# Unused pieces in the SBUF pools: the operands of TensorE at other byte positions against the weights

## The chip, the cores and the metric

The kernel runs on one core of a Trainium2 chip. The metric is the device time of one execution in microseconds (us); for the kernel before it is 1540.58 us, the median of three runs from 1537.99 to 1541.2. Engines are named as in the profile: PE is TensorE (matmuls), PEld its weight loads, DVE VectorE, ACT ScalarE, POOL GpSimd, SP SyncE, which issues the DMAs.

## The reference: one step of a decoder layer

64 sample tokens and 1024 prompt tokens go through one layer with a model width of 1024, in float32:

```
h = RMSNorm(x);  [q|k|v|gu|gv|ga|gb] = h @ w_in
A = sliding-window attention(q, k, v, sinks)          # window 128, 16 heads of 64, 4 KV heads
B = gelu(gu) * (tril(W_s) @ LayerNorm(gelu(gv)) + b)  # chunks of 128 positions, 6 groups
x = x + (sigmoid(ga) * (A @ w_pa) + sigmoid(gb) * (B @ w_pb)) @ w_out
z = RMSNorm(x) @ w_up                                 # 2 x 2816 columns
x = x + (gelu(conv3(z)_a) * conv3(z)_b) @ w_down;  y = RMSNorm(x)
```

Beside y, the newest keys, values, convolution rows and gate rows are returned.

## The kernel before

Every large product is done three times in a reduced-precision form: each float32 operand is split in a high and a low part (`split`, line 39: a cast on ACT, a subtraction on DVE), and PE adds high*high, high*low and low*high into one PSUM bank. So a weight piece has the tiles wh and wl, an activation has th and tl (or hh and hl, mh and ml, oh and ol, s). PE reads the weights as the stationary operand, 128 columns of four bytes in each partition (a weight load, PEld), and the activation as the moving operand, of 256, 288, 320 or 512 columns. Each matmul has a weight load of its own, which runs beside the matmul before it.

The tokens lie in two groups. Group 0 has 576 columns (64 samples and 512 prompt tokens), group 1 has 512. Where both halves of a pair of weight blocks meet both halves of a group, seven products of a Strassen-like scheme take the place of eight (class `Chain`, line 249): each operand tile then holds seven combinations of 288 columns (group 0) or of 256 (group 1), and one product j is four steps kk of three matmuls, twelve in all, with the weights wh[kk], wl[kk] (the matmul at line 295).

The stages in order of time, from the profile's timeline:

- 0 to 115 us, line 511: v and gate columns by tokens; the weights are moving here (tile w2h, w2l, 256 columns), the activations hh and hl stationary.
- 115 to 468 us, line 295: the "pairs" q, k, gu, ga, gb by `Chain`. Group 0's operands are the tiles T0h (288 columns), group 1's the tiles T1h (256). The first three pairs run for group 0 alone, then both groups alternate with each product's weights, and at the end the first three run for group 1 alone.
- 468 to 822 us: attention (lines 1155, 1182, 1206), with the branch and merge products at line 238 between its steps, and then w_out, also line 238. Group 0 runs there in two chunks of 320 and 256 columns, group 1 in one of 512. The operand tiles are in the pools mlp0, act0, hm0 (group 0) and mlp1, act1, hm1 (group 1).
- 822 to 1292 us, line 295 again: the up products. Group 0's operands are the tiles T0 (288 columns), group 1's T1 (256). Three of the 22 pairs of blocks run for group 0 alone at the start, and for group 1 alone among the others.
- 1292 to 1530 us, line 1651: the down products, 288 and 256 columns of one tile in turn, three matmuls each; at the end the final norm and y.

What sets the order: each engine runs its instructions in the order in which the code issues them; the class `Weights` (line 78) issues loads, splits and sums of the weights a fixed number of pieces ahead of PE (`get`, line 219). SBUF is given out by pools: a pool stands as one block of bytes in each partition, opened at the left or (`side="right"`) at the right end of what is free, and its tiles stand one behind another. So an unused tile in a pool moves what is allocated behind it. Where a new tile takes bytes that an older tile had, its first writer waits for the older one's last users.

The lines that the change touches are the pools c1 (line 464), wide (line 496), T0h (tiles at line 648), kv (line 902), mlp1 (line 977), T0 (tiles at line 1407) and T1 (line 1449).

Of the kernel before, what the change touches and what calls it, by code (L numbers as in the profile page):

```python
# [6 lines left out]
F32 = mybir.dt.float32  # L7
# [8 lines left out]
P = 128  # L16
# [18 lines left out]
def layer(tc, a):  # L35
# [3 lines left out]
    def split(hi, lo, src, pin=False):  # L39

        for x in (S.copy(hi, src), V.tensor_sub(lo, src, hi.bitcast(F32))):  # L41
            if pin:
                tc.keep_in_program_order(x)
# [5 lines left out]
    with ExitStack() as top:  # L49
# [191 lines left out]
        W = Weights(top.enter_context(tc.tile_pool(name="wp", bufs=2)), 4, 4)  # L241
        W.sm = top.enter_context(tc.tile_pool(name="sm", bufs=2))

        tx = [{}, {}]
        tops = ExitStack()

# [2 lines left out]
        def right(stack, name, bufs=1):  # L249
            return stack.enter_context(tc.tile_pool(name=name, bufs=bufs, side="right", reuse_waits="tile"))  # L250
# [110 lines left out]
        with ExitStack() as ph1:  # L361
            c1 = ph1.enter_context(tc.tile_pool(name="c1", bufs=1))
# [31 lines left out]
            wide = {}  # L394
# [68 lines left out]

            rstg = [c1.tile([P, len(gr["toks"])], F32, name=f"rst{gr['g']}") for gr in groups]
            lnst = c1.tile([P, 9, 3, 6], F32, name="lnst")
            pso = ExitStack()
            psa = pso.enter_context(tc.tile_pool(name="psa", bufs=7, space=PSUM))

# [25 lines left out]
            gvp = pa0.enter_context(tc.tile_pool(name="gvp", bufs=4))  # L494
            hp1 = pa0.enter_context(tc.tile_pool(name="hs1", bufs=1))
            wide["pool"] = pa0.enter_context(tc.tile_pool(name="wide", bufs=2))
            hp0 = right(hs0o, "hs0")
            rsg = [pool.tile([P, gr["n"]], F32, name=f"rs{gr['g']}") for gr, pool in zip(groups, (c1, hp1))]
            hs = [[], []]
# [123 lines left out]
            t0h, xr = right(th0, "T0h"), right(xro, "xr")  # L623
# [11 lines left out]
            def sums_of(g, kk):  # L635
                x_in(4 * g + kk + 1)
                n2, x = groups[g]["n"] // 2, xin.pop(4 * g + kk)
                for e in range(2):
                    k = kk + 4 * e
                    V.scalar_tensor_tensor(x[:, e], x[:, e], gains[:, 0, k:k + 1], rsg[g], ALU.mult, ALU.mult)  # L640
                t4 = xr.tile([P, 4, 288], F32, name="t", bufs=2)[:, :, :n2]
                combine(t4, *(x[:, e, n2 * h:n2 * h + n2] for e in range(2) for h in range(2)), eng=V)
                return x[:, 0, 0:n2], t4, x[:, 1].rearrange("p (h c) -> p h c", h=2)

            def t0_job(kk):
                def go():
                    first, t4, rest = sums_of(0, kk)
                    txa[0][kk] = th, tl = tuple(t0h.tile([P, 7, 288], F32R, name=f"t{y}{kk}") for y in "hl")
                    split(th[:, 0], tl[:, 0], first)
                    split(th[:, 1:5], tl[:, 1:5], t4)  # L650
                    split(th[:, 5:7], tl[:, 5:7], rest)
                return go

            def t1_job(kk):
# [6 lines left out]

            none = lambda: None
            jobs = [lambda: x_in(0)] + [x for kk in range(4) for x in (t0_job(kk), none)] + [t1_job(kk) for kk in range(4)]
            tokens(1, ("v", 1), lambda i, ps: v_out(1, i, ps), jobs, lambda: stats_tok(1))
            stats_all(1)
# [224 lines left out]
            kvo, kvp = ExitStack(), {}  # L890
# [3 lines left out]
            def operands(gr, kv):  # L894

                def go():
                    if kv == NKV:
                        if gr["g"] == 0:
                            operands(groups[1], 0)()
                        return  # L900
                    g, n = gr["g"], gr["n"]
                    at, nk = ((NS, 512), (448, 640))[g]
                    t = kvp["p"].tile([P, 2, 640], F32R, name="kst", bufs=2)[:, :, :nk]
                    gr["kst"][kv] = t
                    r = 64 * (kv % 2)
                    for o in (0, 64):
                        nc.sync.dma_start(t[o:o + 64].bitcast(F32), kd[kv // 2][r:r + 64, :, at:at + nk])
                    for c in (2 * kv, 2 * kv + 1):
                        q = gr["qt"][c] = kvp["p"].tile([P, 2, 512], F32R, name="q", bufs=4)
                        nc.sync.dma_start(q.bitcast(F32), qd[g][c][:, :, gr["soff"]:n])  # L910
                return go

            def prepare(gr):

                g = gr["g"]
                gr["kvo"] = ExitStack()
                vp = (gr["kvo"].enter_context(tc.tile_pool(name="vv0", bufs=1, reuse_waits="tile")) if g == 0
                      else right(gr["kvo"], "vv1"))
                gr["vst"], gr["dvst"] = {}, {}

                def value(name, src, i):
                    def go():
                        t = gr[name][i] = vp.tile([P, NKV, P], F32R, name=f"{name}{i}")
                        nc.sync.dma_start(t.bitcast(F32), src[i])
                    return go

                vs, ds = (((0, 1, 2), (1, 2, 3)), ((3, 4, 5, 6), (4, 5, 6, 7)))[g]
                return [operands(gr, 0)] * (1 - g) + [value("vst", vd, vs[0])] + [
                    x for i in range(len(ds)) for x in (
                        [value("vst", vd, vs[i])] * (i > 0) + [value("dvst", dvd, ds[i])])] + [operands(gr, 1)]  # L930
# [44 lines left out]
            kvp["p"] = kvo.enter_context(tc.tile_pool(name="kv", bufs=1, reuse_waits="tile"))  # L975
            prep = prepare(groups[0])
            m1 = mo[1].enter_context(tc.tile_pool(name="mlp1", bufs=1, reuse_waits="tile"))
            b_order = [(0, 0), (1, 0), (0, 1), (1, 1)] + [(c, g) for c in range(2, KD) for g in range(2)]
            sgs, bst = {}, {}

# [383 lines left out]
            t0p = right(t0o, "T0")  # L1364
# [38 lines left out]
            def t0_split(kk):  # L1403

                def go():
                    x0, x1, t4 = hx.pop(kk)
                    tx[0][kk] = th, tl = tuple(t0p.tile([P, 7, 288], F32R, name=f"t{y}0{kk}") for y in "hl")
                    split(th[:, 0], tl[:, 0], x0[:, 0:288])
                    split(th[:, 5:7], tl[:, 5:7], x1.rearrange("p (h c) -> p h c", h=2))
                    split(th[:, 1:5], tl[:, 1:5], t4)  # L1410
                return go
# [34 lines left out]
        def pool2(name, bufs, **kw):  # L1446
            return ph2.enter_context(tc.tile_pool(name=name, bufs=bufs, reuse_waits="tile", **kw))

        t1p = pool2("T1", 1)
        up = pool2("up", 2)  # L1450
        pse = ExitStack()
        psu = pse.enter_context(tc.tile_pool(name="psu", bufs=8, space=PSUM, reuse_waits="tile"))
# [437 lines left out]
```

## Time and profile before

| What | Value |
|---|---|
| median of three runs | 1540.58 us |
| the profiled execution | 1540.43 us, its span 1538.7 us, 1.7 us around it |
| PE busy | 1524.6 us, 99% of the span, 11528 matmuls |
| weight loads (PEld) | 1483.3 us, 96% |
| DVE, ACT, POOL busy | 1178.6 us (77%), 851.4 us (55%), 267.8 us (17%) |
| DMA | 289.88 MB, 188 GB/s in the mean |
| line 295, all matmuls | 6384 of the 11528 |

The profile's matmul durations run from the start of a matmul to its end in PSUM, and successive matmuls overlap: one of 256 columns is listed with some 0.28 us, and the next starts some 0.12 us later. What a matmul costs the span is the step from its start to the start of the next, so the steps are read from the timeline's start times, or from a stretch of time divided by the matmuls in it.

### The profile page before, as it was taken

The page shows a single profiled execution, that of the slowest core. Times are in us where ns is not written, and L with a number is a line of the kernel's source. Part 1 is how long each engine was busy: PE and PEld are TensorE (multiplying, and loading weights), DVE is VectorE, ACT ScalarE, POOL GpSimd, SP SyncE. Part 2 cuts the span into 40 slices and gives each one's busy share as a digit, 9 for nine tenths or more (in the row PEclk, how much of TensorE's full clock was granted, in tenths as well). Part 3 has the DMA queues.
Part 4 walks back from the last instruction along what each step waited for, and adds up shares of the span by engine and source line. Part 5 has one row for each costly group of instructions (what it writes and reads, how often), then busy time and mean ns, then how long its engine had stood idle before and what let it go on. Part 6 is the DMA issues. An engine that isn't in the chain of part 4 may idle for free.

```text
span 1538.7 us, 30106 instructions
## 1 busy us (share of the span) xinstructions
PE 1524.6 (99%) x11528; PEld 1483.3 (96%) x11528; DVE 1178.6 (77%) x1897; ACT 851.4 (55%) x1767; POOL 267.8 (17%) x382
## 2 busy tenths in 40 slices
PE   9999999999999999999999999999999999999997
PEld 8999999999998989988989999999999999999997
DVE  7798876755576877979568978898898878775686
ACT  7557666653455775764444554655555556453452
POOL 0001000110030222310234222332142222000002
PEclk9999999999999999999999999999999999999999
DMA  7687446764778757449977423332232216973363
GB/s 244 219 270 260 161 161 218 236 212 142 241 237 285 221 165 252 152 140 312 339 255 267 138 109 113 121 120 93 108 128 100 102 62 224 365 252 96 111 183 123
DMA packets 135231, 289.88 MB, mean 188 GB/s; under 512 B 15536, under 2 KB 36848, under 8 KB 135088
## 3 DMA queue, kind: packets, MB, share of 16 engines
q1 hardware_dynamic: 134944, 287.96, 55.3%
q8 instruction: 90, 1.47, 0.4%
q14 instruction: 53, 0.43, 0.1%
q10 hardware_dynamic: 144, 0.01, 0.0%
HBM read 198.97 MB, written 90.92 MB: 188 GB/s over the span
## 4 chain that ended last, share of the span: by engine, by line
PE 87%; DMA 4%; DVE 3%; issue 3%; ACT 2%; POOL 1%; SPq 0%; POOLq 0%; ACTq 0%; DVEq 0%
PE st L295 45%; PE mm L238 16%; PE dn L1651 13%; PE st L511 6%; PE po L1206 2%; PE sc L1155 2%; PE pt L1182 1%; DMA v<-gvd 1%; POOL x L1714 1%; PE mx L793 1%; DMA wl<-upd 1%; DVE wl L41 1%; DMA kd<-q 0%; DMA x<-xt 0%; ACT wh L41 0%
## 5 line engine op out<-in xcount | busy, mean ns | idle before, releaser
L295 PE MATMUL st<-th,wh 128*128 128x288 f32 (+1 forms) x2128 | 616.9, 290 | 1.6 <-ACT k L274 1.2
L295 PE MATMUL st<-tl,wh 128*128 128x288 f32 (+1 forms) x2128 | 615.3, 289 | 0.0
L295 PE MATMUL st<-th,wl 128*128 128x288 f32 (+1 forms) x2128 | 614.4, 289 | 0.0
L295 PEld LDWEIGHTS st<-th,wh 128*128 128x128 f32 x2128 | 402.8, 189 | 3.1 <-ACT k L274 2.2
L295 PEld LDWEIGHTS st<-th,wl 128*128 128x128 f32 x2128 | 402.8, 189 | 0.0
L295 PEld LDWEIGHTS st<-tl,wh 128*128 128x128 f32 x2128 | 402.7, 189 | 0.0
L41 ACT CAST wh<-wraw 128x512 fp32r<-128x512 f32 (+2 forms) x188 | 129.4, 700 | 92.8 <-PE mm L238 41.4
L1651 PE MATMUL dn<-th,wh 128*128 128x288 f32 (+1 forms) x616 | 177.5, 288 | 0.8 <-ACT zb L321 0.6
L1651 PE MATMUL dn<-th,wl 128*128 128x288 f32 (+1 forms) x616 | 177.3, 288 | 0.2 <-DVE wl L41 0.2
L1651 PE MATMUL dn<-tl,wh 128*128 128x288 f32 (+1 forms) x616 | 177.2, 288 | 0.0
L41 DVE TENSOR_TENSOR wl<-wraw,wh 128x512 fp32r<-128x512 f32 (+2 forms) x188 | 148.2, 802 | 24.8 <-ACT wh L41 22.3
L41 DVE TENSOR_TENSOR wl<-ws,wh 128x512 fp32r<-128x512 f32 x168 | 118.5, 716 | 54.2 <-ACT wh L41 53.4
L41 ACT CAST wh<-ws 128x512 fp32r<-128x512 f32 x168 | 102.5, 621 | 91.7 <-PE st L295 63.4
L1651 PEld LDWEIGHTS dn<-th,wh 128*128 128x128 f32 x616 | 115.8, 188 | 1.2 <-ACT zb L321 0.8
L1651 PEld LDWEIGHTS dn<-th,wl 128*128 128x128 f32 x616 | 115.9, 188 | 0.4 <-DVE wl L41 0.4
L1651 PEld LDWEIGHTS dn<-tl,wh 128*128 128x128 f32 x616 | 115.9, 188 | 0.0
L41 ACT CAST th<-traw 128x544 fp32r<-128x544 f32 (+1 forms) x85 | 54.5, 642 | 52.1 <-PE dn L1651 38.5
L511 PE MATMUL st<-w2h,hh 128*128 128x256 f32 x288 | 81.3, 284 | 1.5 <-ACT hh L46 0.7
L511 PE MATMUL st<-w2l,hh 128*128 128x256 f32 x288 | 81.0, 282 | 0.0
L511 PE MATMUL st<-w2h,hl 128*128 128x256 f32 x288 | 80.3, 282 | 0.2 <-DVE hl L47 0.2
L41 DVE TENSOR_TENSOR tl<-traw,th 128x544 fp32r<-128x544 f32 (+1 forms) x85 | 61.0, 721 | 23.1 <-ACT th L41 22.7
L281 POOL TENSOR_TENSOR z<-kn,k 128x288 f32<-128x288 f32 (+1 forms) x32 | 31.1, 975 | 244.0 <-ACT kn L276 236.6
(271 smaller groups left out, 2941.3 us busy)
## 6 DMA issues: line engine op xcount, KB each, us to landing
wraw<-wt SPq DMA_DIRECT2D x137, 512.0 KB
traw<-td SPq DMA_DIRECT2D x77, 272.0 KB
td<-za SPq DMA_DIRECT2D x22, 544.0 KB
q<-qd SPq DMA_DIRECT2D x16, 512.0 KB
upd<-hl SPq DMA_DIRECT2D x14, 512.0 KB
td<-t SPq DMA_DIRECT2D x11, 544.0 KB
wpart<-wt SPq DMA_DIRECT2D x22, 256.0 KB
qd<-q SPq DMA_DIRECT2D x8, 576.0 KB
```

The lines of the kernel that those rows point to most:

```text
L41: for x in (S.copy(hi, src), V.tensor_sub(lo, src, hi.bitcast(F32))):
L238: PE.matmul(ps[:, lo:lo + c1 - c0], u[:, k, :], v[:, c0:c1], start=(k == 0 and i == 0), stop=(k == nk - 1 and i == 2))
L281: op(to, pick(x, to, lo, hi), pick(y, to, lo, hi))
L295: PE.matmul(ps, u[:, kk, :], v, start=first and kk + i == 0, stop=kk == 3 and i == 2, skip_group_check=True)
L511: PE.matmul(ps, u[:, lo:lo + P], v[:, k, :], start=k + i == 0, stop=k == KD - 1 and i == 2)
L793: PE.matmul(ps[:, P * i:P * i + P], vn[:, i], late["wst"][:, c, :], start=True, stop=True)
L1155: PE.matmul(ps[:, h, o0:256], q, kst[kv][:, e, k0:cur + P], start=e == 0, stop=e == 1)
L1182: PE.transpose(pt[:, h * P:h * P + P], s[:, h, 0:P], ident)
L1206: PE.matmul(po, v[:, kv, :], t, start=e == 0, stop=last)
L1651: PE.matmul(place(m, e), u[:, m, :], v[:, lo:hi], start=new and i + k == 0 and (e == 0 or m % 2 == 0), stop=i == NU - 1 and k == 2, skip_g ...
L1714: G.tensor_mul(xc, xc, rs)
```

## The change: unused pieces in seven pools

A helper `line(pool, n)` allocates a tile of n bytes in each partition that nothing reads or writes. It is called once in each of the pools c1 (96 bytes), wide (64), T0h (32), kv (64), mlp1 (64) and T1 (64), and twice in T0 (96 bytes, behind the tiles of kk = 1 and behind those of kk = 3).

```diff
+        gaps = iter(range(99))
+
+        def line(pool, n):
+
+            pool.tile([P, n // 4], F32, name=f"gap{next(gaps)}", bufs=1)
...
             lnst = c1.tile([P, 9, 3, 6], F32, name="lnst")
+            line(c1, 96)
...
             wide["pool"] = pa0.enter_context(tc.tile_pool(name="wide", bufs=2))
+            line(wide["pool"], 64)
...
                     split(th[:, 5:7], tl[:, 5:7], rest)
+                    if kk == 3:
+                        line(t0h, 32)
...
                     gr["kst"][kv] = t
+                    if g == 0 and kv == 0:
+                        line(kvp["p"], 64)
...
             m1 = mo[1].enter_context(tc.tile_pool(name="mlp1", bufs=1, reuse_waits="tile"))
+            line(m1, 64)
...
                     tx[0][kk] = th, tl = tuple(t0p.tile([P, 7, 288], F32R, name=f"t{y}0{kk}") for y in "hl")
+                    if kk % 2:
+                        line(t0p, 96)
...
         t1p = pool2("T1", 1)
+        line(t1p, 64)
         up = pool2("up", 2)
```

The instructions of all engines, their order and their shapes are the same as before. What differs is where tiles stand. In the built programs every weight piece wh, wl of the pool wp starts at a byte position of 32 modulo 128, before and after. The table gives the moving operand's start minus that of the weights of the same matmul, modulo 128 (the "offset" from here on):

| Matmuls | Columns | Count | Offset before | Offset after |
|---|---|---|---|---|
| pairs, T0h (line 295) | 288 | 1344 | 64 | 32 |
| pairs, T1h (line 295) | 256 | 1344 | 96 | 64 |
| up, T0 of kk = 0 and 1 (line 295) | 288 | 924 | 64 | 0 |
| up, T0 of kk = 2 and 3 (line 295) | 288 | 924 | 64 | 96 |
| up, T1 (line 295) | 256 | 1848 | 0 | 64 |
| line 511, group 0, until 80 us | 256 | 480 | 32 | 64 |
| line 511, group 1, from 80 us | 256 | 384 | 0 | 64 |
| line 238, act0 and hm0 | 320 and 256 | 768 | 96 | 64 |
| line 238, mlp1 and hm1 | 512 | 336 | 96 | 64 |
| line 238, mlp0; act1 | 320 and 256; 512 | 288; 192 | 64 | 64 |
| line 1155, kv (scores) | 256 and 128 | 256 | 0 | 64 |
| line 1206, at0; at1 (values) | 512 | 56; 64 | 32; 64 | 96; 96 |
| line 1651, down products | 288 and 256 | 1848 | 64 | 64 |

Since tiles now overlap other older tiles than before, three DMAs on SP differ in what they wait for. On SP in the down products, the load of the first residual tile x, which takes bytes that belonged to the pool up before (names: x1d are the DRAM tiles of the residual, wraw and traw raw weights and activations, td the DRAM tiles of the gated products). Before:

```order
L131 DMA wraw<-wt 128x512 [waits DMAHW7_49]
L1437 DMA traw<-td_72 128x544 [waits DMAHW0_49,Activation_49]
L131 DMA wraw<-wt 128x1024 [waits DMAHW1_49]
L1639 DMA x_16743<-x1d_57 128x544 [waits DMAHW2_49]
L1639 DMA x_16743<-x1d_58 128x544 [waits DMAHW3_49]
```

With the change:

```order
L131 DMA wraw<-wt 128x512 [waits DMAHW7_49]
L1452 DMA traw<-td_72 128x544 [waits DMAHW0_49,Activation_49]
L131 DMA wraw<-wt 128x1024 [waits DMAHW1_49]
L1655 DMA x_16751<-x1d_57 128x544 [waits DMAHW2_49,PE_49]
L1655 DMA x_16751<-x1d_58 128x544 [waits DMAHW3_49]
```

The first of the four pieces of x now also waits for PE: the last 64 bytes of T1 reach into x's place, so PE must have ended the up products. In return two later loads on SP (the tiles a22 of the down weights, line 441 before) no longer wait for PE.

## The prediction

> **What bounds the kernel now.** I read the page's first two parts and its chain first, then the table of waits, then the timeline and stretches of time for the step from one matmul to the next.
>
> ```profile
> span 1538.7 us, 30106 instructions
> PE 1524.6 (99%) x11528; PEld 1483.3 (96%) x11528; DVE 1178.6 (77%) x1897; ACT 851.4 (55%) x1767; POOL 267.8 (17%) x382
> PEclk9999999999999999999999999999999999999999
> PE 87%; DMA 4%; DVE 3%; issue 3%; ACT 2%; POOL 1%; SPq 0%; POOLq 0%; ACTq 0%; DVEq 0%
> PE st L295 45%; PE mm L238 16%; PE dn L1651 13%; PE st L511 6%; PE po L1206 2%; PE sc L1155 2%; PE pt L1182 1%; DMA v<-gvd 1%; POOL x L1714 1%; PE mx L793 1%; DMA wl<-upd 1%; DVE wl L41 1%; DMA kd<-q 0%; DMA x<-xt 0%; ACT wh L41 0%
> ...
> PE st L295 <- ACT k L274: 1.2, 2, 0.9
> PE st L566 <- DVE c_ones L69: 1.2, 1, 1.2
> ```
>
> PE is busy in 99% of the span at the full granted clock, the chain is 87% PE, and the longest waits of PE sum to 1.2 us each. So the span is a sum of PE's steps, and the change can matter only through their length: it adds no instruction and moves none. A step shorter by 1 ns in all 6384 matmuls of line 295 is 6.4 us.
>
> The timeline in the up products, at the borders between group 1's twelve matmuls (256 columns, offset 0) and group 0's (288, offset 64):
>
> ```profile
> 1087.97 0.28 PE L295 MATMUL st<-th,wh 128*128 128x256 f32 x1
> ...
> 1089.41 0.30 PE L295 MATMUL st<-th,wh 128*128 128x288 f32 x1
> 1089.55 0.30 PE L295 MATMUL st<-tl,wh 128*128 128x288 f32 x1
> ...
> 1091.00 0.28 PE L295 MATMUL st<-th,wh 128*128 128x256 f32 x1
> ...
> 1092.43 0.30 PE L295 MATMUL st<-th,wh 128*128 128x288 f32 x1
> ```
>
> Twelve of 256 columns take 1.44 and 1.43 us, 119.6 ns a step. Twelve of 288 take 1.59 us, 132.5 ns. Nothing waits between them, so these are PE's own steps.
>
> Other offsets are found in other stages. Stretches of time with the matmuls in them (each is in flight for about two steps, so a stretch also counts two that began before it; I take two off):
>
> ```profile
> core 0: us, PE busy (x), PEclk, DMA share, GB/s
> 30.00:50.00 20.00, 20.00 (x173) 1.00 0.69 218
> 85.00:112.00 27.00, 27.00 (x228) 1.00 0.87 296
> 120.00:148.00 28.00, 28.00 (x213) 1.00 0.73 245
> 437.00:467.00 30.00, 30.00 (x253) 1.00 0.88 297
> 681.00:724.00 43.00, 43.00 (x186) 1.00 0.88 304
> 727.00:776.00 49.00, 49.00 (x370) 1.00 0.95 334
> 783.00:821.00 38.00, 38.00 (x164) 1.00 0.69 225
> 1300.00:1480.00 180.00, 180.00 (x1445) 1.00 0.62 204
> ```
>
> - 256 columns, offset 32 (line 511, group 0, first row): 20/171 = 117.0 ns.
> - 256 columns, offset 0 (line 511, group 1, second row): 27/226 = 119.5 ns. The same line, shape and weights as the row before; only the activation tile and its offset differ.
> - 288 columns, offset 64 (T0h alone, third row): 28/211 = 132.7 ns.
> - 256 columns, offset 96 (T1h alone, fourth row): 30/251 = 119.5 ns.
> - 512 columns, offset 64 (act1) and 96 (hm1), the rows from 681 and 783: 43/184 = 233.7 and 38/162 = 234.6 ns.
> - 320 and 256 columns in turn, offset 96 (hm0, from 727): 49/368 = 133.2 ns, 266.3 for the two.
> - 288 and 256 in turn, offset 64 (down products, last row): 180/1443 = 124.7 ns, 249.5 for the two.
>
> The last is split by the timeline; the same 320 and 256 columns at offset 64 (mlp0) stand in the chain of waits as a piece without a gap:
>
> ```profile
> 1390.40 0.28 PE L1651 MATMUL dn<-th,wh 128*128 128x256 f32 x1
> ...
> 1390.75 0.30 PE L1651 MATMUL dn<-th,wh 128*128 128x288 f32 x1
> ...
> 1391.15 0.28 PE L1651 MATMUL dn<-th,wh 128*128 128x256 f32 x1
> ...
> 516.60 3.16 PE mm L238 x24
> ```
>
> Three of 256 in 0.35 us are 116.7 ns, three of 288 in 0.40 us 133.3. With 132.3 for 288 (between 131.7, below, and 132.7) the pair of 249.5 leaves 117.2 for 256 at offset 64, which I take. The mlp0 piece is 3.16/24 = 131.7 ns, 263.3 for the two.
>
> So 256 columns take about 117 ns at offsets 32 and 64, and about 119.5 at 0 and 96. The difference holds in stages with a DMA share from 0.3 to 0.9, so I lay it on the position of the operand against the weights that load beside it.
>
> **The change part by part.**
>
> 1. T1 goes from offset 0 to 64: 1848 x (119.6 - 117.2 = 2.4 ns) = 4.4 us saved.
> 2. T1h goes from 96 to 64: 1344 x 2.3 ns = 3.1 us saved.
> 3. Line 511, group 1, from 0 to 64: 384 x 2.3 = 0.9 us saved. Group 0 goes from 32 to 64, 117.0 to 117.2: nothing.
> 4. Line 238, act0 and hm0, from 96 to 64: 133.2 - 131.7 = 1.5 ns on 768, 1.1 us saved. The 336 of 512 columns: 0.9 ns, 0.3 us.
> 5. Scores and values, 376 matmuls with gaps for the softmax between them: at 2.3 ns each either way 0.9 us at most. I take nothing, since PE runs there with other work to fill in.
>
> Together 9.8 us on the side of the gain, nearly all in stretches in which nothing but PE ends last.
>
> 6. The 288-column operands, 3192 matmuls, leave offset 64, where alone the trace shows them. Their price at 32, 0 and 96 must be bounded. Below nothing: a straight line between 256 columns (117.2) and 320 (263.3 - 117.2 = 146.1) at offset 64 gives 131.7 for 288; they now step by 132.6, so a better offset may give 0.9 ns, 2.9 us saved. Above: all of them pay what 256 columns pay at the worse offsets, 2.4 ns, 7.7 us lost. Nearest rows: at 32, the 256 columns of line 511 are as fast as at 64, so T0h's 1344 cost nothing. At 96 the wider operands pay less than 256 columns: of the 2.9 ns that the pair 320 and 256 pays, 2.3 belong to the 256, and 0.6 to the 320; 512 columns pay 0.9. For 288, between 2.3 and 0.6, I take 1.5 ns, at 0 the same for want of a row: 1848 x 1.5 = 2.8 us lost.
>
> Sum: 9.8 - 2.8 = 7.0 us less. Against the profiled execution, 1540.43, that is 1533.4; it stands 0.15 us under the median, so 1533.6 us.
>
> What feeds PE has to keep up. The stage with the least slack for the weights' splits, and SP's queue where the one new wait stands:
>
> ```profile
> core 0: us, PE busy (x) PEld busy (x) DVE busy (x) ACT busy (x) POOL busy (x), PEclk, DMA share, GB/s
> 832.00:1290.00 458.00, 457.58 (x3623) 456.64 (x3622) 390.30 (x564) 250.43 (x497) 128.78 (x187) 1.00 0.32 118
> ...
> 1311.34 0.46 SPq L131 DMA_DIRECT2D wraw<-wt  x1
> 1311.85 2.35 SPq L1639 DMA_DIRECT2D x<-x1d  x4
> 1314.29 1.27 SPq L131 DMA_DIRECT2D wraw<-wt  x2
> ```
>
> DVE is busy 390.30 of 458 us there, 85%; with a stage shorter by 2 us it is 86%. The load of x, with the loads of wraw queued behind it on SP, is issued at 1311.85, some 20 us after the last up product (1292 us), so its wait for PE has ended by then. It would cost something only if SP came to it before PE ended the up products. The two waits that fall away on SP stand 27 us later and are as free.
>
> **The rivals.**
>
> - *288 columns gain as well* (they were at their worse offset): 9.8 + 2.9 = 12.7 us less, 1527.8. For it: 132.6 lies above the line of the other widths. Against: 0 and 96 are the worse ones for 256.
> - *The offset does nothing*; the steps of 117 and 119.5 belong to stages, tiles or neighbours in time, and the change only renames bytes: 1540.5. For it: no trace here shows one tile at two offsets. Against: three stages at the worse offsets agree within 0.1 ns, and two at the better ones. This is also what a rule would give: the Trainium skill, "TensorE: Matmul & The Clock Gate", section "Step-by-step: what each phase is for", says that PE has two independent read ports into SBUF, and that loading the next weights takes no read bandwidth from the running matmul. By that the sum would be 0; the two stretches of line 511 (117.0 and 119.5 ns) disagree with it.
> - *The gain is lost to the producers*: PE catches up with DVE's splits in the up products, which then ends last there; the 4.4 us of T1 are lost, 1538.0. For it: 85% busy. Against: in this trace PE waits for DVE or ACT in line 295 for hardly over 1 us.
> - *Slower: 288 columns pay much more at 0 and 96 than 256 do.* Place: the up products of group 0, 1848 steps. The first of T0's twelve after a T1 block at offset 0 already takes 0.14 us against 132.5 ns for the mean, some 7 ns more. At 7 ns each 12.9 us are lost against 9.8: 1543.7. It decides from 9.8/1848 = 5.3 ns a step. Against: no row of 256, 320 or 512 columns shows more than 2.5 ns between two offsets.
>
> **How the numbers follow.** The forecast, 1530.5 to 1537, has a chance of 0.52; 288 columns gaining 0.18; no effect 0.10; producers 0.12; slower 0.08. The likeliest time is 1533.6. The range runs from 1526 (the first rival, with 256 columns at 116.7) to 1539 (9.8 against the upper bound of 7.7, or the third rival). Less than 0.2% either way can't be told from no change, so faster means under 1537.5: the forecast, the first rival and half of the third, 0.76, and a little of the second's edge, 0.77. Same: the rest of the third and the second, 0.16. Slower: 0.07.
>
> **What would show it.** In the profile of the changed kernel, twelve matmuls of T1 should take 1.41 us in place of 1.44, a stretch of T1h alone 117.2 ns a step, line 511 from 80 us on 117; the pair 320 and 256 of hm0 263.3. A T0h step of 132.5 and T0 steps of 134 carry term 6; T0 blocks under 1.58 us mean the first rival, 1.66 and over the last. The count of matmuls and PE's waits should stay; a wait of line 295 for wl of over 1 us would be the third. The prediction is wrong if the 256-column steps stay at 119.5, or if 288-column steps change by over 2.5 ns.

## The result and the profile after

The changed kernel takes 1528.58 us (median of four, 1527.77 to 1530.25) against 1539.63 us for the kernel before beside it: 0.993 of it, with a 95% interval from 0.9912 to 0.9947. The change makes it faster by about 11 us. Run again beside other kernels it took 1530.48 us, 0.994 (0.9928 to 0.9953).

Lines of the page, and the longest waits of PE, of the changed kernel:

```profile
span 1526.5 us, 30105 instructions
PE 1512.8 (99%) x11528; PEld 1471.7 (96%) x11528; DVE 1178.1 (77%) x1897; ACT 851.3 (56%) x1767; POOL 268.3 (18%) x382
PE 90%; issue 3%; DVE 2%; ACT 2%; DMA 1%; POOL 1%; SPq 0%; POOLq 0%; DVEq 0%; ACTq 0%
...
PE st L574 <- DVE c_ones L69: 1.2, 1, 1.2
PE st L519 <- ACT hh L46: 1.0, 1, 1.0
```

The same matmuls, and PE's busy time is 11.8 us less: 1512.8 for 1524.6. DVE, ACT and POOL are as busy as before. So the steps are shorter, as the prediction had it. Four stretches of time show where, first of the kernel before (us, PE's busy time with the matmuls in it, clock, DMA share, GB/s):

```profile
84.00:110.00 26.00, 26.00 (x219) 1.00 0.89 299
180.00:295.00 115.00, 115.00 (x913) 1.00 0.54 184
860.00:1225.00 365.00, 365.00 (x2902) 1.00 0.30 110
1300.00:1455.00 155.00, 155.00 (x1244) 1.00 0.63 208
```

and of the changed kernel:

```profile
84.00:110.00 26.00, 26.00 (x223) 1.00 0.86 294
180.00:295.00 115.00, 115.00 (x932) 1.00 0.58 194
860.00:1225.00 365.00, 365.00 (x2925) 1.00 0.29 108
1300.00:1455.00 155.00, 155.00 (x1245) 1.00 0.61 201
```

With two matmuls taken off for those in flight, the step falls in line 511 (84 to 110 us) from 119.8 to 117.6 ns, in the pairs (180 to 295, half 288 and half 256 columns) from 126.2 to 123.7, and in the up products (860 to 1225) from 125.9 to 124.9. It stays in the down products, whose tiles stand where they stood. These four rows serve as the measure in all experiments.

What of it lies in 256 and what in 288 columns, the borders of the blocks of twelve in the changed kernel's timeline tell (start, duration, instruction):

```profile
238.04 0.29 PE L301 MATMUL st<-th,wh 128*128 128x256 f32 x1
...
239.43 0.30 PE L301 MATMUL st<-th,wh 128*128 128x288 f32 x1
...
241.02 0.29 PE L301 MATMUL st<-th,wh 128*128 128x256 f32 x1
...
242.40 0.29 PE L301 MATMUL st<-th,wh 128*128 128x288 f32 x1
...
1076.09 0.28 PE L301 MATMUL st<-th,wh 128*128 128x256 f32 x1
...
1077.49 0.29 PE L301 MATMUL st<-th,wh 128*128 128x288 f32 x1
...
1079.08 0.28 PE L301 MATMUL st<-th,wh 128*128 128x256 f32 x1
...
1080.49 0.30 PE L301 MATMUL st<-th,wh 128*128 128x288 f32 x1
```

T1h's twelve take 1.39 and 1.38 us, 115.4 ns a step, where 119.5 was read before; T1's 1.40 and 1.41, 117.1 ns, for 119.6. The blocks of 288 columns take 1.59 us in both stages, as before. The means over all steps of a tile, taken from the starts in the whole timeline with waits left out, show the same: T1h goes from 119.8 to 114.8 ns, T1 from 119.7 to 117.8, line 511 (group 1) from 120.0 to 117.8; T0h goes from 132.7 to 132.6, T0 from 132.6 to 132.5. Where an experiment below names the steps of a tile, it is this mean.

Two things were not foreseen: T1h gained more than twice as much as T1 although both now stand at offset 64, and the 288 columns kept their steps. T1h's place is 192 modulo 256, T1's 64. So the theories to part: **A**, what counts is the operand's distance from the weights modulo 256, and for 256 columns; **B**, T1h gained through its neighbour T0h, which moved to 32; **C**, the distance modulo 128, and the pairs differ from the up products by something else; **D**, the operand's own byte position, not its distance from the weights; **E**, a period of 512.

### The profile page after: what moved, and what is told of

Same layout as the page of the kernel before. It is cut to its first block, busy times and chain, and to the rows that moved or that the text cites. A ratio compares the mean times of both kernels' runs of the same rounds, so it can differ in the third digit from the quotient of the medians.

```text
span 1526.5 us, 30105 instructions
## 1 busy us (share of the span) xinstructions
PE 1512.8 (99%) x11528; PEld 1471.7 (96%) x11528; DVE 1178.1 (77%) x1897; ACT 851.3 (56%) x1767; POOL 268.3 (18%) x382
## 4 chain that ended last, share of the span: by engine, by line
PE 90%; issue 3%; DVE 2%; ACT 2%; DMA 1%; POOL 1%; SPq 0%; POOLq 0%; DVEq 0%; ACTq 0%
PE st L301 49%; PE mm L238 15%; PE dn L1667 13%; PE st L519 6%; PE po L1219 2%; PE sc L1168 1%; PE pt L1195 1%; POOL x L1730 1%; DVE wl L41 1%; PE mx L803 1%; DMA stg<-sd 1%; ACT s L1185 1%; DMA x<-xt 0%; DMA wraw<-wt 0%; PE po L1126 0%
## 5 line engine op out<-in xcount | busy, mean ns | idle before, releaser
L41 DVE TENSOR_TENSOR wl<-ws,wh 128x512 fp32r<-128x512 f32 x168 | 118.7, 717 | 51.6 <-ACT wh L41 50.7
L1667 PEld LDWEIGHTS dn<-th,wl 128*128 128x128 f32 x616 | 115.9, 188 | 0.4 <-DVE wl L41 0.4
```

The lines of the kernel that those rows point to most:

```text
L1667: PE.matmul(place(m, e), u[:, m, :], v[:, lo:hi], start=new and i + k == 0 and (e == 0 or m % 2 == 0), stop=i == NU - 1 and k == 2, skip_g ...
```

## The experiments

**The 288-column operands put back.**

```diff
-                    if kk == 3:
-                        line(t0h, 32)
...
-                    if kk % 2:
-                        line(t0p, 96)
```

> The change without the pieces in T0h and T0: the 288-column operands stand at offset 64 as before, everything else as in the change. Theory A (the offset counts modulo 256 and for 256 columns only): T1h steps stay at 114.8 ns (113.4 where it runs alone), 288-column steps at 132.5, the time at 1528.6 within 1 us. Theory B (T1h gains more than T1 because its neighbour T0h moved to 32): T1h steps go to about 117.5, the time 3.5 us up, 1532.

```profile
180.00:295.00 115.00, 115.00 (x928) 1.00 0.57 188
860.00:1225.00 365.00, 365.00 (x2924) 1.00 0.31 111
```

1531.36 us, 0.9943 of before (0.9931 to 0.9955). The up products keep their count, 2924 for 2925. In the pairs 928 for 932: T1h's steps rise from 115.1 to 116.1 beside T0h and stay where T1h runs alone (113.4), T0h's fall by 0.2. Over the stretch this is 0.5 ns a step (124.2 for 123.7 with the two in flight off). So most of T1h's gain is its own, against B, but a neighbour effect of some 1 ns is there too. The time is nearer to B's 1532 than to A's 1528.6, but B's T1h steps of 117.5 are not there. It lies 0.9 to 2.8 us above the change's two medians (the second is 1530.48); about 1 us of it is the neighbour effect, and more of it is waits: in this profile PE waited 1.5 and 1.1 us for ACT and 0.9 us for a DMA, in places where the change's first profile has next to nothing:

```profile
PE st L301 <- ACT k L280: 1.9, 2, 1.5
PE st L301 <- ACT kn L282: 1.1, 1, 1.1
```

**The 288-column operands alone moved**, in the kernel before:

```diff
+                    if kk == 3:
+                        line(t0h, 32)
...
+                    if kk % 2:
+                        line(t0p, 96)
```

> The kernel before with the pieces in T0h and T0 alone: only the 288-column operands move, to offsets 32, 0 and 96. Theory A: no step changes by over 0.5 ns, time as before, 1539.6 within 1 us. Theory B: T1h steps fall by about 2.5 ns though T1h stands where it did, 3 to 4 us less. Term 6 of the prediction (1.5 ns more on the up products' 288): 2.8 us more, 1542.4.

```profile
180.00:295.00 115.00, 115.00 (x912) 1.00 0.56 187
860.00:1225.00 365.00, 365.00 (x2900) 1.00 0.30 109
```

1540.43 us, 1.0002 of before (0.9992 to 1.0013). 912 and 2900 for 913 and 2902: no gain and no loss. The tiles did shift against each other, by about the 0.5 ns of theory A or a little more (T0h up by 0.6 ns and T0 by 0.5, T1h beside T0h down by 0.7 and T1 by 0.4), with a sum of nothing. The loss of 2.8 us in the prediction's term 6 isn't there.

**T1 at 192 in place of 64.**

```diff
-        line(t1p, 64)
+        line(t1p, 192)
```

> The change with 192 bytes in T1 in place of 64: T1 stands at offset 192 modulo 256 in place of 64, the same modulo 128. Theory A (modulo 256): T1 steps go from 117.8 to about 114.8, 1848 x 3.0 = 5.5 us less, 1523.1. Theory C (modulo 128; T1h's 114.8 belongs to the stage of the pairs): T1 steps stay at 117.8, time 1528.6.

```profile
180.00:295.00 115.00, 115.00 (x932) 1.00 0.57 190
860.00:1225.00 365.00, 364.90 (x2956) 1.00 0.30 111
```

1525.54 us, 0.9906 of before (0.9893 to 0.9919). 2956 for 2925 in the up products: T1's steps are 114.8 ns, to the tenth what A expected, and the pairs are as in the change. C falls: the two positions are the same modulo 128. By the counts the stage steps by 123.6 ns for 124.9, 4.8 us on its 3696 matmuls (T0's steps take back 0.6 of T1's 5.4); against the change's two medians 3.0 and 4.9 us arrive in the time.

**T1h at 64 in place of 192.**

```diff
+            line(t1h, 128)
```

> The change with 128 unused bytes ahead of T1h's tiles: T1h at offset 64 modulo 256 in place of 192, the same modulo 128. Theory A (modulo 256): T1h steps go from 114.8 to 117.8, 1344 x 3.0 = 4.0 us more, 1532.6. Theories B and C: T1h stays at 114.8, time 1528.6.

```profile
180.00:295.00 115.00, 115.00 (x923) 1.00 0.56 185
860.00:1225.00 365.00, 365.00 (x2926) 1.00 0.30 111
```

1531.64 us, 0.9947 of before (0.9935 to 0.996). 923 for 932 in the pairs; beside T0h the steps are 117.0 for 115.1. This is A's direction, short of its size: where T1h runs alone, at the end of the stage, the mean stays at 114.2, which A does not explain. T1 alone at 64 has 117.8. The timeline there shows that this mean mixes two values:

```profile
456.63 0.28 PE L301 MATMUL st<-th,wh 128*128 128x256 f32 x1
...
457.99 0.28 PE L301 MATMUL st<-th,wh 128*128 128x256 f32 x1
...
458.85 0.38 PE L301 MATMUL st<-th,wh 128*128 128x256 f32 x1 [0.35 <-ACT k L280]
...
459.30 0.28 PE L301 MATMUL st<-th,wh 128*128 128x256 f32 x1
...
460.72 0.28 PE L301 MATMUL st<-th,wh 128*128 128x256 f32 x1
```

Twelve steps take 1.36 us (113.3 ns each) before a wait of PE and 1.42 us (118.3) after it, with the same tiles at the same distance. Of the 20 blocks of twelve of T1h alone, 17 run at the first value and three, those after the wait, at the second. Beside T0h, 16 of 92 blocks run at 113 to 114 ns and 74 at 118; in the change, at 192, it is 80 and 9. So the distance shifts how many blocks run at which value, and here the value changed at a stop of PE.

**The weights moved, the operands not.**

```diff
+        ga = top.enter_context(tc.tile_pool(name="ga", bufs=1))
+        ga.tile([P, 32], F32, name="gapw0", bufs=1)
         W = Weights(top.enter_context(tc.tile_pool(name="wp", bufs=2)), 4, 4)
         W.sm = top.enter_context(tc.tile_pool(name="sm", bufs=2))
+        gb = top.enter_context(tc.tile_pool(name="gb", bufs=1))
+        gb.tile([P, 32], F32, name="gapw1", bufs=1)
...
-            line(m1, 64)
```

> The change with the weights' pool 128 bytes further on, and another 128 unused bytes behind it: all operands stand where they stood modulo 256, the weights do not (the piece in mlp1 is left out for room). T1's offset goes from 64 to 192 modulo 256, T1h's from 192 to 64. Theory A (what counts is the operand's distance from the weights): T1 steps 114.8 ns, T1h steps 117.0; 5.3 us less and 3 us more, about 1526.4. Theory D (the operand's own byte position counts): T1 117.8 and T1h 115 as in the change, 1528.6. Steps of line 511, whose stationary operand is another tile, stay at 117.8 by both.

```profile
84.00:110.00 26.00, 26.00 (x223) 1.00 0.86 292
180.00:295.00 115.00, 115.00 (x921) 1.00 0.57 186
860.00:1225.00 365.00, 364.91 (x2959) 1.00 0.31 111
```

1526.25 us, 0.9907 of before (0.9891 to 0.9922), at A's 1526.4. T1, untouched, goes to 114.4 ns (2959 for 2925), T1h, untouched, to 117.4 (921 for 932), here 117.8 also where it runs alone. Line 511, whose weights-side tile did not move, keeps its 223. D falls: the distance between the two operands is what counts. All weight tiles of the pool wp stand alike modulo 256, so the runs don't tell a matmul's own weights from those of the next one, which load beside it.

**T1 at 320.**

```diff
-        line(t1p, 64)
+        line(t1p, 320)
```

> The change with 320 bytes in T1: offset 320 modulo 512, 64 modulo 256 as in the change. Theory A with 256 as the period: T1 steps 117.8 alone and beside the 288-column ones, time 1528.6. Theory E (the period is 512, and T1h at 320 had 114.2 alone and 117.0 beside): T1 114.2 and 117.0, 1.8 us less, 1526.8.

```profile
860.00:1225.00 365.00, 365.00 (x2925) 1.00 0.30 110
```

1531.33 us, 0.994 (0.9928 to 0.9953). 2925, the change's own count, and 117.8 ns alone and beside T0: the period is 256, E falls.

**The change once more.**

> The change itself once more, timed beside the others, for the comparison with the 288-column operands put back to 64 (1531.4). If these gain 2.6 us by their move (1.0 in T1h's steps, 1.6 in T0's, as the two profiles' steps give), it is 1528.7; if the difference was scatter between chips, 1530 to 1531.

1530.48 us, 0.994 (0.9928 to 0.9953), which is the second expectation, scatter. The 1.6 us that I had laid on T0's steps in the run with 288 put back was, seen by single steps, mostly the one wait for a DMA named there, so that sum was wrong; T0's steps differ by 0.2 ns. In the two stretches the steps here are those of the first profile (932 and 2926 matmuls), but the span is 1528.4 against 1526.5:

```profile
PE st L301 <- ACT kn L282: 1.4, 1, 1.4
```

The wait for kn stands at 311.8 us; the change's first profile does not have it. The end of the pairs differs too: where T1h runs alone, seven of the 20 blocks, from 445.6 us on, run at 118 ns a step, some 1.41 us in place of 1.36; in the first profile none does (114.9 ns in the mean against 113.4). So two runs of one kernel can differ by such waits, and by which of the two values the steps take.

**All 256-column operands at 192.**

```diff
-            line(wide["pool"], 64)
+            line(wide["pool"], 192)
...
-                th, tl = (dnp["t"].tile([P, HT], F32R, name=x, bufs=5) for x in ("th", "tl"))
+                th, tl = (dnp["t"].tile([P, 576], F32R, name=x, bufs=5)[:, :HT] for x in ("th", "tl"))
...
             t_upto(4, 2)
+            line(dnp["t"], 128)
...
-        line(t1p, 64)
+        line(t1p, 192)
```

> The change with every 256-column operand at 192 modulo 256: T1 by 192 bytes as tried, line 511's by 192 in its pool, and the down products' th and tl as tiles of 2304 bytes in place of 2176, so that all their 256-column halves stand at 192 (now half of them stand at 64). Theory A: line 511 from 117.8 to 114.8, 864 x 3.0 = 2.6 us; down products' 256 columns from 117.3 to 116.2 or below, 924 x 1.1 = 1.0 us; with T1's 3.1 us as measured 1521.9. If 192 is good only in line 295: 1525.5.

```profile
84.00:110.00 26.00, 26.00 (x231) 1.00 0.87 290
1300.00:1455.00 155.00, 155.00 (x1237) 1.00 0.60 195
```

1522.22 us, 0.9882 (0.9867 to 0.9897), the fastest median of all. Line 511 gains what A says, 231 for 223 (114.2 ns in group 1, 114.1 in group 0). The down products lose, 1237 for 1245: their 256 columns hardly gain (117.1 for 117.3) and their 288 columns, which now all stand at 64 modulo 256 where half stood at 192, rise from 132.2 to 133.4. With blocks of three in turn, 192 is not worth there what it is worth in blocks of twelve.

**The same with the down products left alone.** The last edit without the tiles of 576 columns and the piece in dnp.

> The change with T1 and line 511's operands at 192 modulo 256, the down products as they were (in the run with all at 192 their 288-column steps rose from 132.2 to 133.4 and took back what line 511 gave). Theory A with that reading: line 511 at 114.2, T1 at 114.8, down products at 117.3 and 132.2; 1.2 us below that run, about 1521.0. If the loss in the down products was something else: 1522.2.

```profile
84.00:110.00 26.00, 26.00 (x231) 1.00 0.90 296
180.00:295.00 115.00, 115.00 (x932) 1.00 0.58 188
860.00:1225.00 365.00, 364.90 (x2956) 1.00 0.31 111
1300.00:1455.00 155.00, 155.00 (x1244) 1.00 0.62 200
```

1524.39 us, 0.9896 (0.988 to 0.9913), 3.4 us over the expectation. The steps are as expected in all four stretches, the time is not: PE now waits for ACT in the pairs five times, the longest at 310 and 321 us:

```profile
PE st L301 <- ACT k L280: 2.5, 4, 1.0
PE st L301 <- ACT kn L282: 0.7, 1, 0.7
```

The chain of waits shows what ACT is late for, the layer norm's vectors v that come back from DRAM (start, length, piece):

```profile
301.96 4.57 DMA v<-gvd
306.63 1.04 ACT v L746
307.70 0.97 DVE v L748
```

The waits sum to 3.2 us, against 0.3 us in that stage in the change's first profile. But the run before has 2.4 us of them (k 1.4, kn 1.0) and is the faster one, so they are not the whole of the miss. Outside the four stretches, group 0 of line 511 steps by 115.9 ns, with about half of its blocks at 118, where the run before has 114.1: 0.9 us on 480 matmuls. The 0.8 us more of waits and this 0.9 us outweigh the 1.2 us won back in the down products. The expectation also started from the median of the run before, whose four times run from 1519.87 to 1524.68, its profiled one being the slowest. The interval overlaps that of the run before, so the two kernels are not told apart by their times.

**Other offsets for 256 columns.**

```diff
-            line(wide["pool"], 64)
+            line(wide["pool"], 32)
...
+            line(t1h, 32)
...
-        line(t1p, 64)
+        line(t1p, 128)
```

> The change with T1 at 128, T1h at 224 and line 511's operands at 32 modulo 256: the offsets of 256 columns not seen yet. By a period of 256 in which 192 is the one good place (114.8, against 117.7 at 64 and 160 and 119.7 at 0 and 96): T1 at 119 to 120, T1h at 117 to 120, line 511 at 117.7. If 128 is as good as 192: T1 at 115. Times: T1 at 119.7 costs 3.6 us, T1h at 119 5 us against the change, 1537.

```profile
84.00:110.00 26.00, 26.00 (x225) 1.00 0.88 297
180.00:295.00 115.00, 115.00 (x919) 1.00 0.54 184
860.00:1225.00 365.00, 365.00 (x2912) 1.00 0.30 109
```

1535.51 us, 0.997 (0.9959 to 0.9981). T1 at 128 steps by 118.7 ns, a little under the 119 to 120 expected; T1h at 224 by 118.5, within its 117 to 120; line 511 at 32 by 116.9, under its 117.7. None is near 115, so 128 is not another good place.

**The 288-column operands put back where all others stand at 192.** The kernel of all but the down products, without the pieces in T0h and T0.

> The first of these three without the pieces in T0h and T0, so the 288-column operands at offset 64 beside 256-column ones at 192. If the 288's place counts by itself: T0's steps up by 0.9 ns as when they were put back in the change, 1.6 us more, and T1h's by 0.9 ns, 1.0 us more: 1523.6. If it counts only through the neighbours' pattern it can go either way by 1 us; if not at all, 1521.0.

```profile
180.00:295.00 115.00, 115.00 (x928) 1.00 0.59 194
860.00:1225.00 365.00, 364.89 (x2948) 1.00 0.30 109
```

1524.59 us, 0.9906 (0.9889 to 0.9922): above all three expectations, as its partner is above its own, and by time not told apart from it. By steps the neighbour effect is there again: T1's rise from 114.8 to 116.0, T1h's beside T0h from 115.1 to 116.1, T0's fall by 0.6, 2948 for 2956 and 928 for 932. By blocks, T1h beside T0h has 24 of 92 at 118 ns and 33 at 115 where its partner has 9 and 3. So where the 288 columns stand matters a little through the 256-column steps beside them; their own steps, if anything, gained.

## Why the prediction was right, and where not

- **What bounds the kernel.** Right: the whole change is in the steps of PE; PE's busy time fell by 11.8 us and the span by 12.2, and the other engines are as busy as before.
- **The direction and the result.** Faster, 11 us for the forecast 7.0, inside the range of 1526 to 1539 but below the 1530.5 to 1537 that was given the most weight (the second timing, 1530.48, lies at its edge). It is nearest to the first rival's 1527.8, by another way than that rival named: 288 columns did not gain. Since that rival set the lower end of the range, it is in part luck that the range holds the time.
- **Term 1, T1: 4.4 us.** 1848 x 1.9 = 3.5 us. The 117.2 ns at offset 64 was the mean of two classes of the down products: by single steps 118.3 at 64 modulo 256 and 116.2 at 192, and T1 came to stand at 64.
- **Term 2, T1h: 3.1 us.** 1344 x 5.0 = 6.7 us, the term that was mis-sized most. The step that failed is the reading of the offset modulo 128, with one price for both tiles (the row read as offset 32 in line 511 stood at 160 modulo 256, and the down products mixed 64 and 192); the runs with T1 at 192 (114.8) and at 320 (117.8) and the moved weights showed a period of 256 with its best place at 192.
- **Terms 3 to 5.** 384 x 2.2 = 0.8 us for 0.9 in line 511. In line 238 the steps of act0 and hm0 fell by 1.5 ns in the mean, 1.1 us as forecast. The 512 columns stayed in hm1 and fell by 2.9 ns in mlp1, 0.4 us. Scores and values changed by under 0.5 us.
- **Term 6, 2.8 us lost.** Nothing lost. The step that failed carried the price of 256 columns over to 288, with a part for the greater width. The means of T0h and T0 lie between 132.2 and 132.8 ns in the runs at the old place and between 132.4 and 133.3 at the new ones (132.6 and 132.5 in the change), and the run with the 288 columns alone moved has the time of before. The errors of terms 2 and 6 add up, by 3.6 and 2.8 us, and term 1's takes 0.9 back.
- **No effect.** Refuted by the moved weights. That run is also the answer to the rule of the Trainium skill, "TensorE: Matmul & The Clock Gate", section "Step-by-step: what each phase is for", by which loading the next weights takes no read bandwidth from the running matmul: with the weights 128 bytes further on, and mlp1's piece left out beside that, T1's steps went from 117.8 to 114.4 ns. That a weight load and a running matmul disturb each other at some distances fits this, but what inside the memory does it was not shown.
- **Producers.** In the change's up products PE does not wait for DVE. In the pairs the waits at 310 and 321 us are older than the change (0.3 for kn and up to 0.9 us for k in the profile before). They come to 1.7 us in its second profile and to between 1.1 and 3.2 in the three runs with line 511 at 192: part of the next gains is lost there, and the chain shown lays it on the layer norm's vectors and ACT, not on the splits that the rival named.
- **SP's new wait.** The x loads are issued at 1298.16 us, some 20 us after the up products' end, so it cost nothing.

Open stay: what sets which of the two values, 113 or 118 ns, a run of steps takes at 64 and 192 (T1h alone at 64 has 17 blocks of 20 at the lower one with its own tile moved, and all at the higher one with the weights moved), and why it changes at some stops of PE and not at others (T1h's wait at the same place in the change's first profile left it as it was); why blocks of three in the down products do not gain from 192; and whether 288 columns have a good distance of their own. A tile of seven times 288 columns is 8064 bytes, 31.5 times 256, so th and tl stand 128 bytes apart modulo 256 and every mean of the Chain's 288 columns mixes two distances.

## What to carry to other kernels

Where a kernel is a row of matmuls with a weight load each and PE never waits, compare the step between starts, not the listed duration, between stages of one shape: a difference of a few ns at the same shape is worth more than any engine off the path, and some unused bytes in a pool may be all it takes. Before a price is carried from one place to another, split the steps by the exact distance and not by a period that was guessed, look at whether a mean mixes two values, and don't carry the price to another width. As the bound falls, look at the small waits that were there before, for they take the next microseconds back.

## What the runs showed of the hardware

With a stationary operand of 128 columns of four bytes, loaded anew for each matmul, the step of 256 columns depended on the moving operand's start minus that of the weights, modulo 256 (tile means over all steps, waits left out):

| Distance modulo 256 | 0 | 32 | 64 | 96 | 128 | 160 | 192 | 224 |
|---|---|---|---|---|---|---|---|---|
| ns a step | 119.7 to 120.0 | 116.9 | 116.5 to 117.9 | 119.8 | 118.7 | 117.7 | 113.9 to 116.0 | 118.5 |
| from | T1, line 511 | line 511 | T1, T1h, line 511 | T1h | T1 | line 511 | T1, T1h, line 511 | T1h |

The spread is some 5 ns, or 4% of a step. At 64 and 192 the means mix blocks of 113 to 115 and of 118 ns: in the change, T1 at 64 has all but one of its 154 blocks at 118, and T1h at 192 has 9 of 92 there beside T0h; moved to 64, T1h has 74. 320 columns moved by 1.4 to 2.4 ns between 96 and 192; 512 columns by 0.1 between 96 and 192 (hm1) and by 2.9 between 96 and 64 (mlp1); 288 columns of T0h and T0 showed no effect clear of the spread between runs (132.2 to 133.3), with two distances in each mean; in the down products they went from 132.2 with 64 and 192 mixed to 133.4 with 64 alone, beside 256 columns that then all stood at 192.
